# The first stage of an encoder layer: four tiles turned by halves, transposes of the identity put in front, and pieces of work moved from GpSimd to VectorE

## The chip, the core and the metric

The kernel runs on one core of a Trainium2 chip, as one launch. The metric is the device time of a run in microseconds (us). Engines are named as the profile names them: PE (TensorE, matmuls and transposes; PEld is its weight load), DVE (VectorE), ACT (ScalarE), POOL (GpSimd) and SP (SyncE, whose queue issues most DMAs). Each engine takes its instructions in a fixed order; one that waits holds up all that stand behind it on that engine.

## The reference

One layer of a bidirectional encoder on an input of 1024 tokens by 1024 features, in float32: a half-step feed-forward block (SwiGLU, inner width 2816), a token mixer (retention in both directions and a 2-D neighbourhood attention), and a second half-step feed-forward block. Only the first feed-forward block matters here:

```python
h = _swiglu(_rms_norm(x, ffn1_pre_norm[l]), ffn1_w_in[l], ffn1_w_out[l])
x = x + 0.5 * _rms_norm(h, ffn1_post_norm[l])

def _rms_norm(x, gain):
    y = xf * lax.rsqrt(jnp.mean(xf * xf, axis=-1, keepdims=True) + RMS_EPS)
    return (y * gain.astype(jnp.float32)).astype(x.dtype)

def _swiglu(x, w_in, w_out):
    g, u = jnp.split(x @ w_in, 2, axis=-1)
    return (jax.nn.silu(g) * u) @ w_out
```

## The kernel before, in words

**Products.** A float32 product is made of three matmuls of "fp32r" pieces: each operand is split into a high part (a cast on ACT, L62) and a low part (source minus high, a subtraction on DVE, L63); `mm3` (L102 to L104) multiplies high by high, low by high and high by low. One product of a 128 x 512 block by a 512-deep operand is four such triples, 12 matmuls of 512 columns.

**Winograd.** The 1024 x 1024 input (transposed) is cut into four quarters, and a product of it by a block of weights is done with seven products instead of eight: with the operands a11, a12, a22 and the sums s1, s2, s3, s4. `Winograd.put` makes them as the tiles come in: tiles 0 to 3 of 128 tokens give a11 (first half of the features, g = 0) and a12 (second half, g = 1); tiles 4 to 7 give a21 (not kept), a22, s1, s2, s3, and at last s4. In the first stage s4 is made on POOL (L308, L309 and the low part L63 on POOL), four times three instructions of 128 x 512.

**The first stage, in its order.** Eight tiles of 128 tokens are loaded (epx, three buffers), squared and summed on ACT (L126), the root is made on POOL (L112), both halves are scaled on DVE (L132, tile tmp), and each half is turned by four 128 x 128 transposes on PE (L141) into a bank pt, of which there are two. Tiles 0 to 3 are turned as they come. Then `Pairs.lead` runs twelve products a11 and a12 for the first six pairs of weight blocks: six pairs are begun so (three stay in PSUM banks, three are copied to the tile lead). Between them, after every second product, tiles 4 to 7 are turned. Weights are loaded into wraw (three buffers) by SP; the list `(3, 4, 5, 0)` gives the low parts of eight of the twelve weight blocks to POOL.

**The pairs.** Then `ffn_in` runs 22 pairs. `Pairs.run` does for pair i: the subtraction t1 (L421) and t2 (L422) of the weight quarters on DVE, and the products p6 (s2), p2 (a12), p7 (s3), p5 (s1), p4 (a22) and p3 (s4) with the additions between them on DVE (L426, L429, L434, L440, L441, L444, L446). For the first six pairs p1 (a11) and p2 (a12) are there already, so PE has five products of 12 matmuls in each of them, and seven afterwards. `OutSums` (the tile tw) loads blocks of the next weights, subtracts them on DVE (L569) and stores them through POOL's queue; `LeftFactors` makes sums on POOL (L488) and stores them.

**What sets the order.** The code is written as a list of operations. A scheduler places them on the engines by their priorities, and `issue_after`/`after` and the dependency named in `behind` tie some of them to another instruction. The order on each engine is fixed when the program is built.

Of the kernel before, what the change touches and what calls it, by code (L numbers as in the profile page):

```python
# [39 lines left out]
class Core:  # L40
# [74 lines left out]
    def norm_T(self, x, gain, t, pool, put, ss=None, tmps=3):  # L115
# [14 lines left out]
        for b in range(2):  # L130
            bs = slice(b * 512, (b + 1) * 512)
            nc.vector.scalar_tensor_tensor(xn[:, bs], x[:, bs], r[:, 0:1], gain[:, bs], op0=ALU.mult, op1=ALU.mult)  # L132

        return lambda: self.flip([xn[:, :512], xn[:, 512:]], t, put)

    def flip(self, halves, t, put, tag="pt", bufs=2):

        for g, h in enumerate(halves):
            pt = self.bank(tag, bufs)
            for j in range(4):  # L140
                self.nc.tensor.transpose(pt[:, j * P:(j + 1) * P], h[:, j * P:(j + 1) * P], self.ident)  # L141
            f = put(t, g, pt.rearrange("p (k t) -> p k t", k=4))
# [111 lines left out]
class Winograd:  # L254
# [6 lines left out]
    def __init__(self, c, pools, tmp, bufs, spill=None):  # L261

        self.c, self.tmp, self.spill, self.eng, self.late = c, tmp, spill, c.nc.gpsimd, ()
# [11 lines left out]
    def put(self, t, g, pt):  # L275
        c, nc = self.c, self.c.nc
        ts = slice((t % 4) * P, (t % 4 + 1) * P)
        if t < 4:
            c.split(*self.part(("a11", "a12")[g], ts), pt)
            return  # L280
# [7 lines left out]
        if g == 0:  # L288
# [4 lines left out]
            nc.vector.tensor_tensor(self.s3, h1, self.a21, ALU.subtract)  # L293
            nc.vector.tensor_tensor(self.s3, self.s3, l1, ALU.add)
# [12 lines left out]
        if not self.late:  # L307
            self.eng.tensor_tensor(s3, h2, s3, ALU.subtract)  # L308
            self.eng.tensor_tensor(s3, s3, l2, ALU.add)  # L309
            return lambda: c.split(*self.part("s4", ts), s3, eng=self.eng)  # L310
# [26 lines left out]
class Pairs:  # L337
# [3 lines left out]
    def __init__(self, c, x, srcs, held, saved=0, ready=None):  # L341
        self.c, self.x, self.srcs, self.held, self.saved, self.ready = c, x, srcs, held, saved, ready
        self.begun = {}
        self.last = None

    def product(self, a, b, eng=None):
        bank = self.c.bank()
        ah, al = self.x.op(a)
        b = b if isinstance(b, list) else self.c.piece(b, eng)
        for k in range(4):  # L350
            self.c.mm3(bank, [p[:, k * P:(k + 1) * P] for p in b], (ah[:, k], al[:, k]), k == 0, k == 3)
        return bank

# [13 lines left out]
    def lead(self, save=None, between=(), on_pool=(), steps=()):  # L367

        n, done = self.held + self.saved, 0
        for i in (*range(self.held, n), *range(self.held)):  # L370
            if i in self.begun:
                continue
            eng = self.c.nc.gpsimd if i in on_pool else None
            if self.ready is None:
# [5 lines left out]
            for a, w in zip(("a11", "a12"), b):  # L380
                ps.append(self.product(a, w, eng))
                done += 1
                if between and (done in steps if steps else done % 2 == 0):
# [23 lines left out]
    def run(self, i, out, done, sums=None):  # L407
# [16 lines left out]
        late = sums() if sums is not None else []  # L424
        c12 = out(2)
        tt(c12, p6, c11, ALU.add)  # L426
# [7 lines left out]
        self.last = tt(c21, p7, c12, ALU.add).ins  # L434
# [6 lines left out]
        done(3, tt(c12, p5, c12, ALU.add))  # L441
# [3 lines left out]
        p3 = self.product("s4", b22)  # L445
# [1083 lines left out]
```

## Time and profile before

| what | value |
|---|---|
| median of three runs | 2256.53 us (2256.5 to 2257.09) |
| the profiled execution: its own time | 2253.41 us |
| its span, first to last instruction | 2251.6 us |
| PE busy | 2203.2 us, 98% of the span |
| DVE busy | 1677.1 us, 74% |
| ACT busy | 979.2 us, 43% |
| POOL busy | 558.6 us, 25% |

The share of PE is an average. A view by stage tells where PE is not busy: in the first 60 us. A row of the timeline gives start and duration in us, the engine, the line, the operation, what it writes and reads, how many equal ones are merged, and in brackets the idle time before it and what ended it. A matmul's duration is its latency; matmuls overlap, so the distance of two starts is what one costs. L12 is line 12 of the kernel.

### The profile page before, as it was taken

The page shows a single profiled execution, that of the slowest core. Times are in us where ns is not written, and L with a number is a line of the kernel's source. Part 1 is how long each engine was busy: PE and PEld are TensorE (multiplying, and loading weights), DVE is VectorE, ACT ScalarE, POOL GpSimd, SP SyncE. Part 2 cuts the span into 40 slices and gives each one's busy share as a digit, 9 for nine tenths or more (in the row PEclk, how much of TensorE's full clock was granted, in tenths as well). Part 3 has the DMA queues.
Part 4 walks back from the last instruction along what each step waited for, and adds up shares of the span by engine and source line. Part 5 has one row for each costly group of instructions (what it writes and reads, how often), then busy time and mean ns, then how long its engine had stood idle before and what let it go on. Part 6 is the DMA issues. An engine that isn't in the chain of part 4 may idle for free.

```text
span 2251.6 us, 30555 instructions
## 1 busy us (share of the span) xinstructions
PE 2203.2 (98%) x10288; PEld 1834.4 (81%) x10288; DVE 1677.1 (74%) x2941; ACT 979.2 (43%) x2062; POOL 558.6 (25%) x695
## 2 busy tenths in 40 slices
PE   6999999999999999999999999999999999999998
PEld 5888888888887878778888888888788888888886
DVE  7998888855788568869875678534898777776576
ACT  6433333344554222248885675303533332234453
POOL 4343434210121134411101222101124242421012
PEclk9999999999999999999999999999999999999999
DMA  4577787577675542357745477778745454547765
GB/s 168 169 241 277 274 296 266 211 231 236 204 237 191 201 168 99 113 190 243 224 160 178 150 225 241 263 264 297 271 169 187 150 181 147 166 152 239 225 207 180
DMA packets 188014, 466.69 MB, mean 207 GB/s; under 512 B 22417, under 2 KB 50193, under 8 KB 187793
## 3 DMA queue, kind: packets, MB, share of 16 engines
q1 hardware_dynamic: 148944, 334.17, 46.4%
q0 software_dynamic: 38912, 130.58, 14.9%
q8 instruction: 81, 1.33, 0.2%
q14 instruction: 77, 0.62, 0.1%
HBM read 325.72 MB, written 143.13 MB: 208 GB/s over the span
## 4 chain that ended last, share of the span: by engine, by line
PE 85%; DVE 9%; issue 2%; DMA 1%; POOL 1%; ACT 1%; SPq 0%; POOLq 0%; DVEq 0%; ACTq 0%
PE ps L104 26%; PE ps L102 26%; PE ps L103 26%; PE pt L102 1%; PE pt L104 1%; PE pt L103 1%; DVE wl L63 1%; PE ps L806 1%; PE pt L825 1%; POOL rstd L112 1%; DVE t L422 1%; DVE tmp L132 1%; DVE xs L540 1%; PE pt L141 0%; DMA wraw<-in_dram 0%
## 5 line engine op out<-in xcount | busy, mean ns | idle before, releaser
L63 DVE TENSOR_TENSOR wl<-wraw,wh 128x512 fp32r<-128x512 f32 x584 | 426.0, 750 | 53.5 <-ACT wh L62 49.8
L62 ACT CAST wh<-wraw 128x512 fp32r<-128x512 f32 x592 | 345.8, 617 | 204.0 <-DVE wraw L442 89.2
L63 DVE TENSOR_TENSOR gl<-graw,gh 128x512 fp32r<-128x512 f32 (+2 forms) x178 | 129.0, 728 | 163.1 <-ACT gh L62 160.1
L102 PE MATMUL ps<-wh,gh 128*128 128x512 f32 x612 | 239.3, 391 | 0.2 <-DVE tmp L244 0.2
L104 PE MATMUL ps<-wh,gl 128*128 128x512 f32 x612 | 237.3, 390 | 2.0 <-DVE gl L63 1.9
L103 PE MATMUL ps<-wl,gh 128*128 128x512 f32 x612 | 238.3, 389 | 0.0
L62 ACT CAST gh<-graw 128x512 fp32r<-128x512 f32 (+2 forms) x178 | 106.6, 602 | 266.5 <-PE ps L103 99.3
L458 ACT ACTIVATE c<-c 128x512 f32<-128x512 f32 x88 | 55.7, 633 | 265.6 <-DVE c L429 192.5
L104 PEld LDWEIGHTS ps<-wh,gl 128*128 128x128 f32 x612 | 114.7, 188 | 27.1 <-DVE gl L63 3.2
L102 PEld LDWEIGHTS ps<-wh,gh 128*128 128x128 f32 x612 | 114.9, 188 | 24.8 <-DVE tmp L244 1.4
L103 PEld LDWEIGHTS ps<-wl,gh 128*128 128x128 f32 x612 | 114.9, 188 | 23.3
L62 ACT CAST wh<-t 128x512 fp32r<-128x512 f32 x58 | 36.1, 622 | 191.2 <-DVE t L422 178.0
L530 POOL TENSOR_TENSOR q<-q,gain 128x512 f32<-128x512 f32 x22 | 33.5, 1542 | 333.2 <-ACT ps L529 318.5
L102 PE MATMUL ps<-a11h,wh 128*128 128x512 f32 x280 | 111.7, 399 | 0.7 <-ACT a11h L62 0.7
L104 PE MATMUL ps<-a12h,wl 128*128 128x512 f32 x280 | 109.6, 391 | 1.9 <-DVE wl L63 1.9
L104 PE MATMUL ps<-a11h,wl 128*128 128x512 f32 x280 | 110.5, 395 | 0.0
L102 PE MATMUL ps<-a12h,wh 128*128 128x512 f32 x280 | 110.4, 394 | 0.0
L103 PE MATMUL ps<-a11l,wh 128*128 128x512 f32 x280 | 110.2, 394 | 0.0
L102 PE MATMUL ps<-a22h,wh 128*128 128x512 f32 x280 | 109.8, 392 | 0.0
L103 PE MATMUL ps<-a12l,wh 128*128 128x512 f32 x280 | 109.2, 390 | 0.0
L104 PE MATMUL ps<-a22h,wl 128*128 128x512 f32 x280 | 109.1, 390 | 0.0
L103 PE MATMUL ps<-a22l,wh 128*128 128x512 f32 x280 | 109.0, 389 | 0.0
(368 smaller groups left out, 5997.2 us busy)
## 6 DMA issues: line engine op xcount, KB each, us to landing
wraw<-in_dram SPq DMA_DIRECT2D x204, 512.0 KB, 4.5
tw<-in_dram SPq DMA_DIRECT2D x88, 256.0 KB, 3.4
t<-tw POOLq DMA_DIRECT2D x88, 256.0 KB, 4.2
wraw<-t SPq DMA_DIRECT2D x40, 512.0 KB, 3.7
g0s<-cmb POOLq DMA_DIRECT2D x44, 256.0 KB, 5.4
graw<-g0s SPq DMA_DIRECT2D x44, 256.0 KB, 3.1
g1s<-cmb POOLq DMA_DIRECT2D x44, 256.0 KB, 3.9
graw<-g1s SPq DMA_DIRECT2D x44, 256.0 KB, 2.8
```

What stands on the lines that cost most here:

```text
L62: a = nc.scalar.copy(h, src)
L63: self.last = a, (eng or nc.vector).tensor_tensor(l, src, hf, ALU.subtract)
L102: mm(ps, a[0], b[0], start=start, stop=False)
L103: mm(ps, a[0], b[1], start=False, stop=False)
L104: return mm(ps, a[1], b[0], start=False, stop=stop)
L112: self.nc.gpsimd.tensor_tensor(r[:, :n], ms, self.mhalf[:, :n], ALU.pow)
L132: nc.vector.scalar_tensor_tensor(xn[:, bs], x[:, bs], r[:, 0:1], gain[:, bs], op0=ALU.mult, op1=ALU.mult)
L422: tt(t2, b22, t1, ALU.subtract)
L458: a = nc.scalar.activation(gate[j], gate[j], AF.Silu) if j < 2 else None
L530: (eng or c.nc.gpsimd).tensor_tensor(h if out is None else out, h, self.post[:, b * 512:(b + 1) * 512], ALU.mult)
L540: nc.vector.scalar_tensor_tensor(x[:, bs], h, r[:, 0:1], x[:, bs], op0=ALU.mult, op1=ALU.add)
L806: nc.tensor.matmul(bv, q[:, rg * P:(rg + 1) * P], k, start=n == 0, stop=n == 1)
```

## The change

The instructions of the first feed-forward block up to about its seventh pair are changed; all that follows stands in the same order on every engine.

- At the start the first tile is loaded before the gain. 52 transposes of the identity are written ahead of the first tile, and 6 after each of the first three: 70, all into one bank pt that nobody reads (`warm`).
- The first halves of tiles 0 to 3 are scaled and turned first, into four banks of the kind ps (which six products share otherwise); the second halves follow (`early`, `rest`).
- These four banks are kept (`whole`) until tiles 4 to 7 come: s3 starts from the bank with one subtraction (L311) in place of two (before: L293, L294).
- The tiles have four buffers (before: three). The loads of tiles 5 to 7 are written ahead of the second weight block's load. Tiles 6 and 7 are normalised only when tiles 4 and 5 have been turned.
- POOL makes no low part and no s4 any more: all low parts go to DVE, s4 of tiles 4 and 5 to DVE inside pair 0, and s4 of tiles 6 and 7 to DVE inside pair 1 (`s4s`, from s2, with three operations in place of two).
- p3 of pair 0 (s4) is taken out of pair 0 and done after p5 of pair 1 (`hold`, `held`, `tail`).
- Tiles 4 to 7 are turned after products 3, 5, 7 and 9.

In all PE has 70 instructions more, DVE 18 more (8 low parts of weights, 14 for s4, 4 fewer for s3), POOL 20 fewer; ACT and SP have as many as before.

```diff
-        for b in range(2):
+        def scale(b):
             bs = slice(b * 512, (b + 1) * 512)
             nc.vector.scalar_tensor_tensor(xn[:, bs], x[:, bs], r[:, 0:1], gain[:, bs], op0=ALU.mult, op1=ALU.mult)
+        if early:
+            scale(0)
+            self.turn(xn[:, :512], t, 0, put, "ps", 6)
+            def rest():
+                scale(1)
+                self.turn(xn[:, 512:], t, 1, put)
+            return rest
...
+            if g == 0 and self.whole is not None:
+                self.whole[t] = pt
...
-            nc.vector.tensor_tensor(self.s3, h1, self.a21, ALU.subtract)
-            nc.vector.tensor_tensor(self.s3, self.s3, l1, ALU.add)
+            if self.whole is not None:
+                nc.vector.tensor_tensor(self.s3, self.whole.pop(t - 4), self.a21, ALU.subtract)
...
-            self.eng.tensor_tensor(s3, h2, s3, ALU.subtract)
-            self.eng.tensor_tensor(s3, s3, l2, ALU.add)
-            return lambda: c.split(*self.part("s4", ts), s3, eng=self.eng)
...
-        self.last = tt(c21, p7, c12, ALU.add).ins
+        e = tt(c21, p7, c12, ALU.add)
+        self.last = e.ins
+        with c.after((e,)):
+            for f in hold or ():
+                f()
+            if held is not None:
+                held[1]()
...
-        p3 = self.product("s4", b22)
-        done(2, tt(c12, p3, c12, ALU.add))
+        w = c.piece(b22)
+        def tail():
+            p3 = self.product("s4", w)
+            done(2, tt(c12, p3, c12, ALU.add))
...
-        flips = []
-        for t in range(TT):
-            xt = ep.tile([P, D], F32, tag="epx", name="epx", bufs=3)
-            nc.sync.dma_start(xt, x[t * P:(t + 1) * P, :])
-            flips.append(c.norm_T(xt, g, t, ep, wx.put, tmps=4))
-            if t < 4:
-                flips.pop()()
-        fin.lead(lambda: leads.tile([P, 512], F32, tag="lead", name="lead", bufs=6), flips, (3, 4, 5, 0))
+        spin = c.bank("pt", 2)
+        def warm(n):
+            for _ in range(n):
+                nc.tensor.transpose(spin[:, :P], c.ident, c.ident)
+        xs = [load(0)]
+        nc.sync.dma_start(g, g1a)
+        halves = []
+        warm(52)
+        for t in range(4):
+            halves.append(norm(t, xs[t]))
+            warm(6 if t < 3 else 0)
+            xs.append(load(t + 1))
+        fin.fetch(3, 0)
+        for f in halves:
+            f()
+        fin.fetch(3, 1)
+        xs += [load(t) for t in range(5, TT)]
...
+        fin.lead(lambda: leads.tile([P, 512], F32, tag="lead", name="lead", bufs=6), flips, steps=(3, 5, 7, 9))
```

**First place: SP and ACT at the start.** The names: epx is a tile of tokens, wraw a block of weights as loaded, wh its high part, a11h the high part of the first operand, ps and pt banks. Before, on SP, two weight blocks follow the first three tiles, and a third one the fourth:

```order
L1149 DMA epx_169<-in_0_dram 128x1024
L1149 DMA epx_198<-in_0_dram 128x1024
L1149 DMA epx_223<-in_0_dram 128x1024
L79 DMA wraw_317<-in_2_dram 128x1024
L79 DMA wraw_392<-in_2_dram 128x1024
L1149 DMA epx_248<-in_0_dram 128x1024 [waits DMAHW1_49,DVE_49,Activation_49]
L79 DMA wraw_459<-in_2_dram 128x1024
```

Now, on SP:

```order
L1208 DMA epx_293<-in_0_dram 128x1024
L79 DMA wraw_312<-in_2_dram 128x1024
L1208 DMA epx_310<-in_0_dram 128x1024 [waits DMAHW0_49,DVE_49,Activation_49]
L1208 DMA epx_356<-in_0_dram 128x1024 [waits DMAHW2_49,DVE_49,Activation_49]
L1208 DMA epx_358<-in_0_dram 128x1024 [waits DMAHW3_49,DVE_49,Activation_49]
L1208 DMA epx_360<-in_0_dram 128x1024 [waits DMAHW1_49,DMAHW4_49,DVE_49,Activation_49]
L79 DMA wraw_410<-in_2_dram 128x1024
L79 DMA wraw_491<-in_2_dram 128x1024
```

The second weight block (wraw_410) stands behind the loads of tiles 4 to 7, each of which waits until DVE has scaled the tile four before it. And on ACT, now:

```order
L62 CAST wh_352<-wraw_312 128x512
L62 CAST a11h_237<-ps_232 128x4x128 [waits PE_49]
L62 CAST a11h_237<-ps_257 128x4x128 [waits PE_49]
L62 CAST a11h_237<-ps_280 128x4x128 [waits PE_49]
L62 CAST wh_413<-wraw_410 128x512 [waits DMAHW2_49]
L62 CAST a11h_237<-ps_303 128x4x128 [waits PE_49]
L62 CAST a12h_324<-pt_319 128x4x128 [waits PE_49]
```

The high part of the fourth tile's first half (from ps_303), which the first product needs, stands behind the high part of the second weight block.

**Second place: DVE between pair 0 and pair 1.** c0, c1 and gt are the results of pair 0; wraw_802 and wraw_804 (before) or wraw_845 and wraw_847 (now) are the weights of pair 1, and t2 is what its first product p6 reads. Before:

```order
L434 TENSOR_TENSOR c1_682<-ps_713,gt_683 128x512 [waits PE_49]
L421 TENSOR_TENSOR wraw_802<-wraw_804,wraw_802 128x512 [waits DMAHW2_49,DMAHW1_49]
L422 TENSOR_TENSOR t2_806<-wraw_804,wraw_802 128x512 [waits DVE_49]
L431 TENSOR_TENSOR wraw_804<-wraw_804 128x512
L442 TENSOR_TENSOR wraw_802<-wraw_802,t2_806 128x512 [waits DVE_49]
L440 TENSOR_TENSOR gt_683<-ps_731,c1_682 128x512 [waits PE_49]
L441 TENSOR_TENSOR gt_683<-ps_731,gt_683 128x512
L63 TENSOR_TENSOR wl_812<-t2_806,wh_811 128x512 [waits Activation_49]
```

Now:

```order
L460 TENSOR_TENSOR c1_731<-ps_762,gt_732 128x512 [waits PE_49]
L330 TENSOR_TENSOR cmb_435<-a12h_324,cmb_435 128x512
L330 TENSOR_TENSOR cmb_516<-a12h_324,cmb_516 128x512
L331 TENSOR_TENSOR cmb_435<-cmb_435,a12l_325 128x512 [waits DVE_49]
L331 TENSOR_TENSOR cmb_516<-cmb_516,a12l_325 128x512 [waits DVE_49]
L472 TENSOR_TENSOR gt_732<-ps_790,c1_731 128x512 [waits PE_49]
L63 TENSOR_TENSOR s4l_783<-cmb_435,s4h_782 128x4x128 [waits Activation_49]
L63 TENSOR_TENSOR s4l_783<-cmb_516,s4h_782 128x4x128 [waits Activation_49]
L473 TENSOR_TENSOR gt_732<-ps_790,gt_732 128x512
L479 TENSOR_TENSOR c1_731<-ps_810,c1_731 128x512 [waits DVE_49,PE_49]
L444 TENSOR_TENSOR wraw_845<-wraw_847,wraw_845 128x512 [waits DMAHW6_49,DMAHW1_49]
L445 TENSOR_TENSOR t2_849<-wraw_847,wraw_845 128x512 [waits DVE_49]
```

The subtractions for pair 1 stood right behind the sum with p7 of pair 0 (L434); now they stand behind the sum with p4 (L479, bank ps_810). On PE the product that followed p4, p3 of pair 0, is now done inside pair 1, so p6 of pair 1 follows p4 of pair 0.

**Third place: SP between pairs 2 and 3.** wraw_1055 and wraw_1057 (before), wraw_1126 and wraw_1128 (now) are the weights of pair 3; tw are blocks for the sums of the next weights, whose buffers come free when a store of POOL's queue (DMASW) has landed. Before:

```order
L79 DMA wraw_1055<-in_2_dram 128x1024 [waits DMAHW2_49,DMAHW5_49,DVE_49,Activation_49]
L504 DMA graw_4216<-g0a11_78 128x512 [waits DMAHW6_49,DMASW0_49]
L79 DMA wraw_1057<-in_2_dram 128x1024 [waits DMAHW7_49,DMAHW3_49,DVE_49]
L564 DMA tw_1142<-in_3_dram 128x512 [waits DMAHW0_49,DMASW2_49,DVE_49]
L564 DMA tw_1143<-in_3_dram 128x512 [waits DMAHW1_49,DMASW3_49]
L79 DMA wraw_1190<-in_2_dram 128x1024 [waits DMAHW4_49,DVE_49,Activation_49]
L564 DMA tw_1144<-in_3_dram 128x512 [waits DMASW4_49]
L564 DMA tw_1145<-in_3_dram 128x512 [waits DMASW6_49]
```

Now:

```order
L79 DMA wraw_1126<-in_2_dram 128x1024 [waits DMAHW6_49,DVE_49]
L622 DMA tw_1213<-in_3_dram 128x512 [waits DMAHW7_49,DMASW2_49,DVE_49]
L622 DMA tw_1214<-in_3_dram 128x512 [waits DMAHW0_49,DMASW3_49]
L622 DMA tw_1215<-in_3_dram 128x512 [waits DMAHW1_49,DMASW4_49,DVE_49]
L622 DMA tw_1216<-in_3_dram 128x512 [waits DMAHW2_49,DMASW6_49]
L79 DMA wraw_1128<-in_2_dram 128x1024 [waits DMAHW3_49,DVE_49]
```

The second weight block of pair 3 stood ahead of the four tw; now it stands behind them.

104 lines of the change are left out of this document (77 added, 27 removed).

## The prediction

> **What bounds the kernel now.** I read the busy shares by stage first, then PE's timeline for the holes, then what stands ahead of each hole on DVE and SP. The columns of the first view: stretch and its length, then busy time (and instructions) of PE, PEld, DVE, ACT and POOL, granted clock, DMA share, GB/s.
>
> ```profile
> 10.00:20.00 10.00, 4.29 (x17) 2.69 (x16) 8.92 (x12) 7.64 (x18) 8.89 (x8) 1.00 0.73 270
> 20.00:30.00 10.00, 9.32 (x36) 7.51 (x35) 8.09 (x12) 7.50 (x18) 4.53 (x5) 1.00 0.54 164
> 30.00:40.00 10.00, 8.84 (x45) 7.09 (x43) 8.54 (x14) 5.84 (x13) 2.36 (x3) 1.00 0.47 153
> 40.00:50.00 10.00, 6.23 (x32) 4.98 (x32) 8.26 (x14) 6.00 (x12) 5.25 (x3) 0.99 0.16 53
> 61.00:136.00 75.00, 75.00 (x333) 62.08 (x332) 71.96 (x101) 27.89 (x48) 30.62 (x35) 1.00 0.57 191
> ```
>
> Up to 50 us PE has holes. From 61 to 136 us it has none (75.00 of 75), but DVE is busy for 71.96 of the same 75: PE is fed with almost nothing to spare. The change does its good in the first stretch and moves 18 DVE instructions, and several orders, into the second. Now PE's holes:
>
> ```profile
> 19.61 1.97 PE L141 MATMUL pt<-ident,tmp 128*128 128x128 f32 x8 [2.30 <-DVE a12l L63]
> 23.55 0.77 PE L103 MATMUL ps<-a11l,wh 128*128 128x512 f32 x1
> 24.55 0.63 PE L102 MATMUL ps<-a11h,wh 128*128 128x512 f32 x1
> 24.98 0.63 PE L103 MATMUL ps<-a11l,wh 128*128 128x512 f32 x1
> 30.05 1.03 PE L141 MATMUL pt<-ident,tmp 128*128 128x128 f32 x8
> 41.25 0.65 PE L141 MATMUL pt<-ident,tmp 128*128 128x128 f32 x4 [2.41 <-ACT cmb L290]
> 49.68 0.96 PE L141 MATMUL pt<-ident,tmp 128*128 128x128 f32 x4 [2.52 <-ACT cmb L290]
> 50.86 0.63 PE L102 MATMUL ps<-a11h,wh 128*128 128x512 f32 x1
> 53.37 0.39 PE L102 MATMUL ps<-a12h,wh 128*128 128x512 f32 x1
> 53.60 0.39 PE L103 MATMUL ps<-a12l,wh 128*128 128x512 f32 x1
> 67.92 0.39 PE L102 MATMUL ps<-s2h,wh 128*128 128x512 f32 x1
> ```
>
> The second matmul of the first product starts at 23.55, the 145th (the end of the twelve lead products, the start of pair 0) at 67.92. At full clock a matmul costs 53.60 - 53.37 = 0.23 us; behind an idle time of 2.52 us it costs 24.98 - 24.55 = 0.43, as it did at the start (0.63 latency in place of 0.39), until 53.37. So a hole of 2.5 us costs itself and then seven matmuls at 0.2 more, 1.4 us; the one of 2.41 did not. A transpose costs about (30.05 row) 0.1 us warm, (19.61 row) 0.2 cold.
>
> **The start.** SP's queue and the loads, issue by issue:
>
> ```profile
> 0.74 0.38 SPq L1145 DMA_DIRECT2D gpre<-in_dram  x1
> 1.18 1.36 SPq L1149 DMA_DIRECT2D epx<-in_dram  x3
> 5.46 0.63 ACT L126 ACTIVATE tmp<-epx 128x512 f32<-128x512 f32 x1 [3.45 <-DMA epx<-in_dram]
> 7.88 0.63 ACT L126 ACTIVATE tmp<-epx 128x512 f32<-128x512 f32 x1 [1.08 <-DMA epx<-in_dram]
> 9.14 0.63 ACT L126 ACTIVATE tmp<-epx 128x512 f32<-128x512 f32 x1
> 2.59 1.05 SPq L79 DMA_DIRECT2D wraw<-in_dram  x2
> wraw<-in_dram SPq DMA_DIRECT2D x1, 512.0 KB, 7.8
> wraw<-in_dram SPq DMA_DIRECT2D x2, 512.0 KB, 8.1
> 20.88 0.33 SPq L1149 DMA_DIRECT2D epx<-in_dram  x1
> 21.30 0.38 SPq L79 DMA_DIRECT2D wraw<-in_dram  x1
> wraw<-in_dram SPq DMA_DIRECT2D x1, 512.0 KB, 4.4
> ```
>
> Now tile 0 is first and lands about 4.1 (0.74 plus what the gain took, an estimate from the 5.46 of the second load less 1.4 for one load). The rows of a DMA's bytes give the median from issue to landing in the window of that issue (7.8 for the weight block issued at 2.59, 8.1 for it and the next together). Tile 3 is the fifth load behind three tiles and the gain; the fifth of before landed near 10.4 (2.59 + 7.8). Squares of a tile 1.26 (9.14 - 7.88), root and scaling about 2, and on DVE the scaling of tile 2 and a low part in between: the second half of tile 3 is scaled at about 15.8. Only then SP may issue tile 7's load (15.9), and behind it the second weight block (16.3). That lands 4.4 later (the row of 21.30, a weight block right behind a tile) at 20.7; its cast on ACT takes 0.6, and only behind it comes the cast of tile 3's first half, 0.6: first product at 22.0, its second matmul (one low part on DVE later) at 22.7. Against 23.55 that is **-0.9**. The four first halves are turned by about 15; they then lie for 6 us behind one cast that waits for a weight block. Without that wait the first product could start near 16.
>
> The 70 transposes: 52 at 0.2 to 0.1 us are 10.4 to 5.2 us from about 2.4 (identity made). They cost nothing, because PE waits for tiles then, but they buy nothing either: between 16 and 22 PE is idle for longer than the 2.52 us that cost the clock before, so the first product is cold again, as now.
>
> The Trainium skill (TensorE: Matmul & The Clock Gate, Part 4: PE-mode transpose) says that transposes do not count as activity for the gate; Part 1 says that one idle window of about 3.4 us drops the clock. By the first, 70 transposes never warm PE; by the second it is cold at 22 anyhow. The trace agrees with the second as far as 2.52 us of idle time dropped it; the first no row here can show.
>
> **The lead products.** From the second matmul to the 145th are 143 matmuls. Before: 143 x 0.227 = 32.5, 36 transposes 3.9, the holes 2.41 + 2.52, the cold clock some 3: 44.4 = 67.92 - 23.55. Now 40 transposes (4.3), a cold start (2.2), no two holes if DVE keeps up: per tile of 4 to 7 it has 11 instructions at 0.60 (6.6 us) for two products and eight transposes on PE (6.3 us), so some 0.3 is lost: 39.3. The 145th matmul starts at 62.0: **-5.9** in all. If the cover is gone, the holes of 4.9 stay; that is one end.
>
> **Pair 0 to pair 1.** DVE's rows around this place, and POOL's against DVE's:
>
> ```profile
> 73.67 0.68 DVE L434 TENSOR_TENSOR c<-ps,gt 128x512 f32<-128x512 f32 x1
> 74.30 0.69 DVE L421 TENSOR_TENSOR wraw<-wraw 128x512 f32<-128x512 f32 x1
> 75.03 0.69 DVE L422 TENSOR_TENSOR t<-wraw 128x512 f32<-128x512 f32 x1
> 75.64 0.68 DVE L431 TENSOR_TENSOR wraw<-wraw 128x512 f32<-128x512 f32 x1
> 12.04 2.95 POOL L63 TENSOR_TENSOR wl<-wraw,wh 128x512 fp32r<-128x512 f32 x2
> 12.18 1.68 DVE L132 SCALAR_TENSOR_TENSOR tmp<-epx,rstd,gpre 128x512 f32<-128x512 f32 x1
> 13.78 0.68 DVE L63 TENSOR_TENSOR a12l<-pt,a12h 128x512 fp32r<-128x512 f32 x1
> ```
>
> Before, t2 of pair 1 was ready at 75.7, with p5, p4 and p3 of pair 0 (3 x 12 x 0.227 = 8.2 us) still ahead of PE. Now the subtractions stand behind the sum with p4, and p6 of pair 1 follows p4 at once on PE. From p4's last matmul: 0.3 until DVE has it, then three DVE instructions (sum, t1, t2) at 0.6 to 0.7, a cast of 0.6, hand-overs of 0.1 to 0.2: **+3.0**, whatever DVE's backlog. Being longer than 2.52 it costs the clock too: **+1.4**.
>
> **DVE's ledger and pair 2.** DVE gets 18 x 0.60 = 10.8 us more. It gets back what POOL took: while POOL runs, a DVE instruction with both operands in SBUF took 1.68 in place of 0.75 (12.18), one that reads PSUM 0.68 (13.78). Twenty POOL instructions fewer are worth 0 to 20 x 0.93 = 18.6; the two about cancel.
>
> The Trainium skill (GPSIMD Engine Reference, 1. Specifications) says that POOL's SBUF interfaces are shared with VectorE, so that the two hold each other up. The stretched rows agree (1.68 against 0.68); by that rule alone the relief would be at its upper end and DVE free sooner, 18.6 - 10.8 = 7.8 us.
>
> But the work comes in worse places. In pair 1 the six operations for s4 and two low parts stand ahead of pair 2's subtractions, and in pair 2 twelve DVE instructions (sums of pair 0's tail, pair 1's ends, four tw) stand ahead of the low part that p7 needs. 12 x 0.6 = 7.2, one or two stretched by POOL to about 1.2 to 1.7, less the 5 us that p6 and what is left of p3 keep PE busy: 2.2 to 4, I take **+3.0**, and the clock again, **+1.4**.
>
> **Pairs 3 to 5.** The ticks of DVE (its first subtraction of a pair), and SP:
>
> ```profile
> 87.78 0.68 DVE L421 TENSOR_TENSOR wraw<-wraw 128x512 f32<-128x512 f32 x1
> 102.28 1.82 DVE L421 TENSOR_TENSOR wraw<-wraw 128x512 f32<-128x512 f32 x1
> 94.63 0.33 SPq L79 DMA_DIRECT2D wraw<-in_dram  x1
> 100.71 0.92 SPq L564 DMA_DIRECT2D tw<-in_dram  x2
> 101.81 0.33 SPq L79 DMA_DIRECT2D wraw<-in_dram  x1
> 102.19 6.48 SPq L564 DMA_DIRECT2D tw<-in_dram  x2
> ```
>
> Pair 3's second weight block was issued at 94.63, ahead of the four tw. Now it waits for all four, the last of which went at 102.19 + 6.48 = 108.7 less its own 0.3. With 4.4 to land it comes at 110 to 113, when DVE's tick would have been at 102 to 109. Per pair that is 0 (PE still has products) to 6.5 (108.3 - 101.81); with half a pair in hand I take 2, for pairs 3, 4 and 5 **+6**. Afterwards each pair has seven products, 7 x 12 x 0.227 = 19.1 us of PE, and DVE falls behind no more; nothing that follows is reordered, and PE has no slack to win the loss back.
>
> **Sum.** -5.9 + 3.0 + 1.4 + 3.0 + 1.4 + 6 = +8.9. The profiled execution took 2253.41 (span 2251.6 and 1.8 around it), so 2262.3; the median of the runs is 3.1 above it: **2265.4 us**.
>
> **The rivals.**
> - *Only the head counts* (faster). DVE's relief is at the upper end (18.6 - 10.8 = 7.8 us gained), so pair 2 and pairs 3 to 5 cost nothing, and only pair 1's wait stays: -5.9 + 3.0 + 1.4 = -1.5; with the first product at 16 besides, -7.5: 2249 to 2255. For it: the stretched rows. Against: tick and load order, which POOL's relief doesn't touch.
> - *Gain and loss cancel.* Pairs 3 to 5 at 0 and pair 2 at half: about +1, 2257.
> - *Transposes don't warm, and delay.* The 19.61 row shows transposes at 0.2 us each, behind ten microseconds in which PE did scattered transposes. If a run of transposes alone leaves the clock where it was, all 70 and the real ones run at 0.2: 52 until 13, then 18 and 24 more until 22. The first product comes 1 to 1.5 later, and there is one window more at half clock: +2.5, 2268. For it: the 0.2 of the 19.61 row behind 12 us of scattered transposes. Against: that PE was mostly idle then. The rule of the Trainium skill named above (TensorE: Matmul & The Clock Gate, Part 4: PE-mode transpose) would have it so.
> - *The doing does nothing*: the bank that nobody reads is one of two pt banks; it is free when tile 1's second half needs it (about 15), so no price.
>
> **How the numbers follow.** Forecast 0.58, transposes that don't warm 0.19, cancel 0.11, only the head 0.12. What a measurement of this kernel can tell from no change is 0.2%, 4.5 us: faster 0.12, same 0.11, slower 0.77. The forecast's terms have the ends -0.9 (both old holes stay) or -7 at the head, 4.4 for pair 1, 1 to 5.5 for pair 2, 0 to 12 for pairs 3 to 5: about +2 to +16 without all ends at once, 2258 to 2273 for itself. The whole range takes the cancelling case in: 2256 to 2274.
>
> **What would show it.** In the trace after: PE idle from about 15 to 21 with ACT waiting for a weight block; matmul 145 near 62; an idle time of 3 us ahead of the first s2 product of pair 1 released by the cast of t2; one near pair 2's s3 product released by a low part; DVE's first subtraction of pairs 3 to 5 waiting for a load. Wrong it is if PE has no holes between 65 and 140 us, or if the first product starts before 18.

## The result, and the profile after

The changed kernel takes 2272.97 us (median of 6 runs, 2268.36 to 2276.02), the kernel before 2256.52 us: the ratio is 1.0079, with a 95% interval of 1.0067 to 1.0092, that is 15 to 21 us slower. In a second set of runs the ratio was 1.0085 (1.0071 to 1.0099). The forecast was slower by 8.9 us: the direction was right, the size half of what came.

The profiled execution has a span of 2271.3 us, 19.7 more than before. First the busy shares by stage of the changed kernel, with the same columns as in the prediction:

```profile
10.00:20.00 10.00, 4.49 (x36) 3.54 (x33) 7.08 (x13) 3.35 (x9) 1.53 (x2) 0.96 0.80 253
20.00:30.00 10.00, 5.45 (x17) 4.18 (x18) 4.60 (x8) 5.07 (x10) 0.00 (x0) 0.53 0.52 171
30.00:40.00 10.00, 10.00 (x49) 8.34 (x49) 8.83 (x16) 8.00 (x19) 1.47 (x2) 1.00 0.40 120
40.00:50.00 10.00, 9.48 (x48) 7.72 (x47) 9.52 (x18) 7.08 (x15) 0.86 (x1) 1.00 0.55 197
61.00:136.00 75.00, 65.39 (x266) 51.20 (x264) 61.49 (x94) 22.63 (x37) 13.98 (x20) 0.95 0.42 145
```

The change did what it was meant to do between 30 and 50 us: PE is busy for 19.5 of 20 us there (before 15.1). It lost on both sides of that: at 20 to 30 us PE is busy for 5.45 us at a clock of 0.53, and from 61 to 136 us for 65.39 of 75, where it had no hole before. DVE is not fuller there but emptier, 61.49 in place of 71.96. That speaks against DVE's amount of work as the cause; the experiments test it. PE's timeline names the larger holes:

```profile
24.50 0.79 PE L102 MATMUL ps<-a11h,wh 128*128 128x512 f32 x1 [8.39 <-ACT a11h L62]
25.34 0.79 PE L103 MATMUL ps<-a11l,wh 128*128 128x512 f32 x1
79.10 0.50 PE L102 MATMUL ps<-s2h,wh 128*128 128x512 f32 x1 [2.81 <-ACT wh L62]
104.35 0.72 PE L104 MATMUL ps<-s3h,wl 128*128 128x512 f32 x1 [2.75 <-DVE wl L63]
117.97 0.50 PE L102 MATMUL ps<-s2h,wh 128*128 128x512 f32 x1 [1.75 <-ACT wh L62]
133.93 0.50 PE L102 MATMUL ps<-s2h,wh 128*128 128x512 f32 x1 [1.43 <-ACT wh L62]
151.78 0.50 PE L102 MATMUL ps<-s2h,wh 128*128 128x512 f32 x1 [3.01 <-ACT wh L62]
```

A good ruler for what follows is the start of the s2 product of each pair: the same instruction in every kernel, and read off PE's timeline. The table gives it in us for the kernel before, and for the others the difference to it. (In the changed kernel pair 1's s2 has one product fewer ahead of it, p3 of pair 0, which is 2.7 us of PE. So its entry for pair 1 reads 2.7 too low.)

| s2 of pair | 0 | 1 | 2 | 3 | 4 | 5 | 6 | 7 to 11 |
|---|---|---|---|---|---|---|---|---|
| before, at | 67.92 | 81.54 | 95.14 | 108.74 | 122.34 | 135.94 | 152.70 | |
| changed | -2.67 | -2.44 | +2.67 | +9.23 | +11.59 | +15.84 | +17.46 | +17.46 |
| changed, second set | -2.67 | -2.43 | +1.26 | +7.62 | +9.62 | +13.55 | +15.06 | +15.06 |

So the head gained 2.7 us, pairs 0 and 1 together lost 5.3, pair 2 and the wait behind it 6.6 (4.8 and the hole of 1.75 ahead of pair 3), pairs 3 to 5 another 8.2, and from pair 6 on nothing changes any more. That is 17.5 of the 19.7 us. The other 2.2 us came in between two table loads on ACT, which stood 17.1 apart and then 19.3. Before:

```profile
1181.51 1.28 ACT L1325 ACT_TABLE_LOAD   x1
1638.90 1.28 ACT L458 ACT_TABLE_LOAD   x1
```

And in the changed kernel:

```profile
1198.63 1.28 ACT L1416 ACT_TABLE_LOAD   x1
1658.17 1.28 ACT L508 ACT_TABLE_LOAD   x1
```

Nothing is reordered there. The profiles of ten other kernels of this study also lose 0.9 to 5.7 us in that stretch against this one execution of before, even the kernel before with 70 transposes more; so it is read as a difference between executions and not as an effect of the change, though no second profile of the kernel before shows it. The 17.5 us agree with the ratio of the runs (0.0079 x 2256.5 = 17.8). In the second set they do not: its trace has 15.1 us in the first stage, its ratio gives 19.2, and 4.2 lie in the stretch between the two table loads. So a trace and the medians can differ by some 4 us here.

**The head.** The timeline of SP and ACT, changed kernel:

```profile
3.13 0.44 SPq L79 DMA_DIRECT2D wraw<-in_dram  x1
9.23 6.96 SPq L1208 DMA_DIRECT2D epx<-in_dram  x4
16.24 2.69 SPq L79 DMA_DIRECT2D wraw<-in_dram  x3
23.34 0.62 ACT L62 CAST wh<-wraw 128x512 fp32r<-128x512 f32 x1 [9.68 <-DMA wraw<-in_dram]
23.86 0.58 ACT L62 CAST a11h<-ps 128x512 fp32r<-128x512 f32 x1
```

SP holds the second weight block behind tiles 4 to 7 until 16.24. ACT waits 9.68 us for it, and the last first half of tiles 0 to 3 (a11h), which PE had turned by 15.2, is cast behind it. The view of the DMA issues of that moment gives what the load took, in us from issue to landing:

```profile
wraw<-in_dram SPq DMA_DIRECT2D x1, 512.0 KB, 7.1
```

**Pairs 2 to 5.** DVE's timeline: what pair 2's low parts took, and the first subtractions of pairs 3, 4 and 5:

```profile
103.01 3.60 DVE L63 TENSOR_TENSOR wl<-wraw,wh 128x512 fp32r<-128x512 f32 x2
106.54 1.87 DVE L477 TENSOR_TENSOR wraw<-wraw,t 128x512 f32<-128x512 f32 x1
115.79 0.69 DVE L444 TENSOR_TENSOR wraw<-wraw 128x512 f32<-128x512 f32 x1 [3.55 <-DMA wraw<-in_dram]
131.28 0.69 DVE L444 TENSOR_TENSOR wraw<-wraw 128x512 f32<-128x512 f32 x1 [2.89 <-DMA wraw<-in_dram]
149.60 0.69 DVE L444 TENSOR_TENSOR wraw<-wraw 128x512 f32<-128x512 f32 x1 [3.96 <-DMA wraw<-in_dram]
```

All three first subtractions wait for a load, as forecast, and each hole of PE ahead of an s2 product (1.75, 1.43, 3.01) follows one of them.

**What the transposes did.** The view of the tile pt in two windows, 1.4 to 5.0 us and 5.5 to 9.2 us (shortest, median, longest duration in ns):

```profile
L1228 PE MATMUL pt<-ident x17: 421/421/474, 1.4 to 4.8; 128*128 128x128 f32 x17
L1228 PE MATMUL pt<-ident x34: 272/273/384, 5.3 to 9.0; 128*128 128x128 f32 x34
```

And the busy time by stretch when they are over (columns as above):

```profile
16.20:19.40 3.20, 0.00 (x0) 0.00 (x0) 1.98 (x4) 0.00 (x0) 0.00 (x0) 0.96 0.84 261
19.40:24.40 5.00, 0.00 (x0) 0.00 (x0) 0.41 (x1) 1.06 (x3) 0.00 (x0) 0.50 0.80 276
```

The transposes do warm the clock: after some 4 us of them a transpose takes 273 ns in place of 421, and twice as many are done in the same time (17 and then 34, in windows of 3.6 and 3.7 us). The column of the granted clock does not show this step: it reads 1.00 for 1.5 to 4.9 us too, so at the very start it says nothing of a cold PE. But PE then has nothing to do for 8.4 us, the granted clock falls to 0.50 at about 19.1 (the 0.96 of the first row), and the first product runs at half speed. The Trainium skill (TensorE: Matmul & The Clock Gate, Part 4: PE-mode transpose) says that the gate's full clock does not engage for transposes, since they do not count as PE being busy in the same way. These rows, 421 and then 273 ns, do not agree.

### The profile page after: what moved, and what is told of

Same layout as the page of the kernel before. It is cut to its first block, busy times and chain, and to the rows that moved or that the text cites. A ratio compares the mean times of both kernels' runs of the same rounds, so it can differ in the third digit from the quotient of the medians.

```text
span 2271.3 us, 30683 instructions
## 1 busy us (share of the span) xinstructions
PE 2216.5 (98%) x10358; PEld 1843.5 (81%) x10358; DVE 1677.2 (74%) x2959; ACT 979.3 (43%) x2062; POOL 529.1 (23%) x675
## 5 line engine op out<-in xcount | busy, mean ns | idle before, releaser
L63 DVE TENSOR_TENSOR wl<-wraw,wh 128x512 fp32r<-128x512 f32 x592 | 432.9, 752 | 65.1 <-ACT wh L62 61.3
```

The lines of the kernel that those rows point to most:

```text
L63: self.last = a, (eng or nc.vector).tensor_tensor(l, src, hf, ALU.subtract)
```

## The experiments

Each row is the difference of the s2 starts to the kernel before, as above, and then the ratio of the runs to the kernel before with its interval.

| kernel | pair 0 | 2 | 3 | 4 | 5 | 7 | ratio |
|---|---|---|---|---|---|---|---|
| changed | -2.7 | +2.7 | +9.2 | +11.6 | +15.8 | +17.5 | 1.0079 (1.0067 to 1.0092) |
| early_load | -7.0 | -0.8 | +5.3 | +7.6 | +11.7 | +13.6 | 1.0077 (1.0064 to 1.0089) |
| sums_on_pool_queue | -4.3 | +1.1 | +7.7 | +8.4 | +10.7 | +11.0 | 1.0053 (1.0040 to 1.0065) |
| p3_in_pair_0 | -2.6 | 0.0 | +2.0 | +4.4 | +5.7 | +6.1 | 1.0021 (1.0011 to 1.0030) |
| no_transposes | -11.2 | -5.8 | +0.7 | +2.3 | +6.4 | +8.3 | 1.0049 (1.0035 to 1.0062) |
| first_sums_on_dve | -2.7 | +2.4 | +9.1 | +9.1 | +12.1 | +12.4 | 1.0064 (1.0052 to 1.0076) |
| before_with_transposes | +7.6 | +7.6 | +7.6 | +7.6 | +7.6 | +7.6 | 1.0050 (1.0037 to 1.0063) |
| before_pool_work_on_dve | -4.8 | -1.5 | -1.5 | -1.4 | -1.4 | -1.4 | 0.9994 (0.9985 to 1.0003) |
| two_mended_again | -11.2 | -7.5 | -5.3 | -2.9 | -1.7 | -1.3 | 0.9992 (0.9983 to 1.0001) |
| three_mended | -11.2 | -7.6 | -7.6 | -7.2 | -4.9 | -4.5 | 0.9983 (0.9974 to 0.9991) |
| four_mended | -10.8 | -8.3 | -3.8 | -1.5 | -1.5 | -1.6 | 0.9991 (0.9982 to 0.9999) |

The theory under test is that of the prediction: the time is a sum of separate waits, each of them made by what stands in front of something else in a queue. Its main rival: DVE, full from 61 to 136 us before, got 18 instructions too many, and every gain elsewhere is lost to that.

**early_load**: the load alone.

```diff
-                g = self.c.raw(self.srcs[i][0])
+                g = self.raws[i] if i in self.raws else self.c.raw(self.srcs[i][0])
...
+        fin.raws[4] = c.raw(fin.srcs[4][0])
         xs += [load(t) for t in range(5, TT)]
```

> The changed kernel with one load moved: the second weight block (the lead products' second pair) is issued behind tile 4 instead of behind tiles 5, 6 and 7; its two casts then stand ahead of tile 3's first half on ACT, and pair 0's first subtractions come a little earlier on DVE. All that stands behind pair 0 keeps its order. Theory (a sum of separate waits): the 8.4 us in which PE waited for one cast go; first product at about 17 instead of 24.5, warm from the start because PE has turned tiles until 16; the 145th matmul at 58 to 60 instead of 65.3, and all holes behind it stay: 5 to 7 us less than the changed kernel, ratio to the kernel before 1.0048 to 1.0057. Rival (DVE's work is the bound of the whole stage): tiles 4 to 7 come no sooner, the 145th matmul stays near 64, gain under 2 us, ratio 1.007 or more.

Measured: 2270.92 us, ratio 1.0077. The first product starts at 17.18, as the theory had it, and pair 0 comes 4.3 us earlier, not 5 to 7. PE's timeline shows why it is less:

```profile
17.18 0.51 PE L102 MATMUL ps<-a11h,wh 128*128 128x512 f32 x1 [1.10 <-ACT a11h L62]
20.01 0.80 PE L103 MATMUL ps<-a11l,wh 128*128 128x512 f32 x1 [2.33 <-DVE a11l L63]
```

After one matmul PE waits 2.33 us for a low part of a11, which now stands behind the low parts of the weight block on DVE, and the clock is lost in spite of the transposes (0.51 over 19.8 to 23.2 us). In the trace 3.9 of the 4.3 us are still there at pair 7. The run times cannot tell 3.9 us from nothing here (the two intervals overlap almost entirely), so by time this one is inconclusive. By the trace the rival is wrong in its place: tiles 4 to 7 do come sooner, and what is gained at the head is kept.

**no_transposes**: the 70 transposes left out, which no other instruction reads.

```diff
-        warm(52)
...
-            warm(6 if t < 3 else 0)
```

> The changed kernel without the 70 transposes of the identity. Nobody reads them, but the planner counted their time: without them it puts the second and third weight blocks ahead of tiles 5 to 7 by itself and places the first products earlier on ACT and DVE. Theory (the transposes buy nothing, PE is idle long enough behind them to lose the clock): first product at about 16 to 17, its first matmuls at half clock, 145th matmul at 57 to 61; 4 to 7 us less than the changed kernel, ratio 1.0045 to 1.006. Rival (the transposes warm the clock and that is worth something): first product no earlier or colder than now, time the same as or above the changed kernel, ratio 1.0079 or more.

Measured: 2264.90 us, ratio 1.0049, 8 us less than the changed kernel by the medians; in the traces 8.5 at pair 0 and 9.2 at pair 7, so what the head gains is kept. SP's timeline:

```profile
9.29 2.29 SPq L1208 DMA_DIRECT2D epx<-in_dram  x2
11.63 0.90 SPq L79 DMA_DIRECT2D wraw<-in_dram  x2
17.87 0.99 SPq L1208 DMA_DIRECT2D epx<-in_dram  x2
```

and PE's:

```profile
15.88 0.50 PE L102 MATMUL ps<-a11h,wh 128*128 128x512 f32 x1 [1.18 <-ACT a11h L62]
```

Without them the planner, the scheduler that places the instructions, puts the second and third weight blocks ahead of tiles 6 and 7 by itself, and the first product starts at 15.88, 8.6 us earlier. The granted clock is still 1.00 there (13.8 to 17.0 us) and 0.50 from 17.2 to 20.4 us. The transposes are no work that anybody waits for. What they cost comes from the order: with them in the program other instructions are placed elsewhere. That the planner counts their time is only a reading; no run shows how it decides.

**before_with_transposes**: the same 70 in the kernel before, and nothing else.

```diff
+        spin = c.bank("pt", 2)
...
+        warm(52)
...
             if t < 4:
                 flips.pop()()
+                warm(6 if t < 3 else 0)
```

> The kernel before with the 70 transposes of the identity alone (52 ahead of the tiles, 6 behind each of the first three). Theory (they cost through the planner, which counts them and so moves other work): the first product starts at 26 to 34 instead of 22.3, since casts of weights and squares of later tiles now stand ahead of the first tiles on ACT; some of it comes back because tiles 4 to 7 are then ready early; 145th matmul at 70 to 76 (before 67.9), 3 to 9 us slower, ratio 1.0013 to 1.004. Rival (transposes are free and warm the clock): first product at about 22 at full clock, 1.5 us gained, ratio 0.9993 to 1.

Measured: 2265.04 us, ratio 1.0050, above what was expected. PE's timeline:

```profile
22.57 1.12 PE L141 MATMUL pt<-ident,tmp 128*128 128x128 f32 x4 [11.14 <-DVE a11l L63]
34.17 0.79 PE L102 MATMUL ps<-a11h,wh 128*128 128x512 f32 x1
```

PE waits 11.14 us among the tiles and starts its first product at 34.17. Of these 11.9 us, 7.6 are left at pair 0 and stay to the end of the first stage. The runs show 3 to 4 us more; in the profile they lie in the stretch between 1181 and 1639 us named above, and why the runs have them too is open.

**p3_in_pair_0**: the product p3 of pair 0 and s4 of all four tiles put back into pair 0, still all on DVE.

```diff
             held.append(end)
+            for f in held:
+                f()
+            held = None
             continue
```

> The changed kernel with the product p3 of pair 0 and all of s4 put back at the end of pair 0 (DVE still makes all of s4, none on POOL). Theory (p3 was the cover under which DVE prepares pair 1): the hole of 2.81 us ahead of pair 1's s2 product goes, 5.3 us with the clock behind it, and the one of 2.75 us in pair 2, 4.7 us, since pair 2's low part no longer stands behind twelve other instructions: 8 to 12 us less than the changed kernel, ratio 1.0025 to 1.0045, below that if pairs 3 to 5 also gain from it. Rival (18 more DVE instructions are too many wherever they stand): p3 now waits for the last low part of s4, a hole of 3 to 5 us at the end of pair 0, gain under 4 us, ratio above 1.006.

Measured: 2259.55 us, ratio 1.0021, 11.4 us less than the changed kernel at pair 7. PE's timeline has one hole in its place, and DVE's first subtraction of pair 3 comes 7.2 us earlier:

```profile
78.38 0.50 PE L103 MATMUL ps<-s4l,wh 128*128 128x512 f32 x1 [1.76 <-DVE s4l L63]
```

```profile
108.55 0.69 DVE L444 TENSOR_TENSOR wraw<-wraw 128x512 f32<-128x512 f32 x1 [2.86 <-DMA wraw<-in_dram]
```

All the 18 instructions are still on DVE, so the rival falls here. At pair 1 the trace tells the cover from the order: DVE's two subtractions for pair 1 come even later than in the changed kernel (the first at 78.84 in place of 76.94), and yet PE has no hole, because p3 runs meanwhile. So the missing cover made the hole of pair 1. Behind it the edit changes more than one thing: s4 no longer stands ahead of pair 2 on DVE, and on SP a weight block now goes at 102.21, behind two tw loads instead of four. How the gain in pairs 2 and 3 is shared among these is not shown.

**before_pool_work_on_dve**: the ledger by itself. In the kernel before, eight low parts and the 12 instructions for s4 go from POOL to DVE.

```diff
-        self.c, self.tmp, self.spill, self.eng, self.late = c, tmp, spill, c.nc.gpsimd, ()
+        self.c, self.tmp, self.spill, self.eng, self.late = c, tmp, spill, c.nc.vector, ()
...
-        fin.lead(lambda: leads.tile([P, 512], F32, tag="lead", name="lead", bufs=6), flips, (3, 4, 5, 0))
+        fin.lead(lambda: leads.tile([P, 512], F32, tag="lead", name="lead", bufs=6), flips, ())
```

> The kernel before with its 20 POOL instructions of the first stage (8 low parts of weights, 12 of s4) on DVE, no other edit; p3 of pair 0 stays in its pair. Theory (what DVE gets and what it is no longer held up by POOL cancel): lead products a little earlier (145th matmul at 63 to 66 instead of 67.9), p3 of pair 0 waits 1 to 3 us for s4, and from pair 1 on as before: -4 to +2 us, ratio 0.998 to 1.001. Rival (DVE is full from 61 to 136 us, so 12 us more work there is 12 us more time): ratio 1.003 to 1.005.

Measured: 2253.81 us, ratio 0.9994: no difference by time, 1.4 us gained in the trace at pair 7. Pair 0 starts 4.8 us earlier and loses 3.3 of it, but not where it was expected: p3 waits for nothing. PE waits ahead of pair 0 (a row of its timeline, then the busy time of the stretch behind it):

```profile
63.12 0.80 PE L102 MATMUL ps<-s2h,wh 128*128 128x512 f32 x1 [3.04 <-ACT wh L62]
62.70:69.50 6.80, 6.38 (x14) 4.63 (x15) 4.49 (x8) 4.51 (x7) 0.00 (x0) 0.50 0.01 2
```

On DVE t2 of pair 0 stands behind low parts and a sum for s4 there, its cast comes late, and behind the hole the clock is 0.50 for 6.8 us, which are the 3.3 (half of 6.8 is 3.4). So the 20 instructions are felt by PE at one place, and in all the earlier start pays for it.

**sums_on_pool_queue**: tw loads of the second and third set on POOL's queue.

```diff
...
-            self.c.nc.sync.dma_start(t, src[:, k * 512:(k + 1) * 512])
+            (self.c.nc.gpsimd if k in (2, 3) and self.side else self.c.nc.sync).dma_start(t, src[:, k * 512:(k + 1) * 512])
```

> The changed kernel with the second and third set of four tw loads issued from POOL's queue instead of SP's, so that no weight block waits behind them; a few DVE and ACT instructions of pairs 3 to 5 come in another order. Theory (a load queued behind the tw loads): DVE's first subtractions of pairs 3, 4 and 5 wait for no load; the holes ahead of those pairs' s2 products (1.75, 1.43, 3.01 us and the clock behind them) go, so that the 500th matmul, now 17.5 us behind the kernel before, is 8 to 10 behind; 7 to 9 us less than the changed kernel, ratio 1.0040 to 1.0050. Rival (DVE is full there): the subtractions come as late as now for want of DVE, gain under 3 us, ratio 1.0065 or more.

Measured: 2265.11 us, ratio 1.0053, less than expected. Of the 6.4 us that it is ahead at pair 7, 1.6 are there before the edit can act (the second weight block landed in 5.4 us in place of 7.1, and the first product starts at 22.90 in place of 24.50). Pairs 4 and 5 gain 4.8, pair 3 nothing: its first subtraction still waits, 3.56 us.

```profile
114.23 0.69 DVE L444 TENSOR_TENSOR wraw<-wraw 128x512 f32<-128x512 f32 x1 [3.56 <-DMA wraw<-in_dram]
127.89 0.69 DVE L444 TENSOR_TENSOR wraw<-wraw 128x512 f32<-128x512 f32 x1 [1.06 <-DMA wraw<-in_dram]
144.45 0.69 DVE L444 TENSOR_TENSOR wraw<-wraw 128x512 f32<-128x512 f32 x1 [0.73 <-DMA wraw<-in_dram]
```

SP's waits from 100 to 150 us (what it waited for, total, times, longest) tell what holds pair 3's load when no tw stands ahead of it:

```profile
SPq L79 <- DVE wl L63: 46.7, 6, 26.3
```

The load waits for a buffer: there are three for weight blocks, and they come free when DVE has made pair 2's low parts. In the changed kernel too the last of the four tw had been issued by 108.1, and the weight block went only at 109.87.

**first_sums_on_dve**: POOL's first four sums (L546) on DVE.

```diff
...
-        c, eng, j = self.c, self.c.nc.gpsimd, i // 2
+        c, eng, j = self.c, self.c.nc.vector if i == 1 and self.dst is LeftFactors.side else self.c.nc.gpsimd, i // 2
```

> The changed kernel with POOL's first four sums (of pairs 0 and 1, 1.3 to 1.5 us each, at 100 to 108 us) on DVE, so that POOL holds up no DVE instruction there. In the changed kernel the three low parts and the subtraction of pair 2 at 103 to 108 us took 7.9 us in place of 2.4. Theory (part of the unforeseen loss in pairs 2 and 3 is DVE held up by POOL at the very place where pair 2's weight buffers are freed for pair 3's loads): the stretched instructions take 0.6 to 0.7 each; the low part that p7 of pair 2 waits for comes 1 to 2 us later (four sums ahead of it), but the buffers come free 2 to 3 us earlier, the first subtraction of pair 3 is 2 to 3 us earlier and its hole of 1.75 us goes; in all 1 to 4 us under the changed kernel, ratio 1.0062 to 1.0078. Rival (four DVE instructions more are 2.4 us more where DVE is the bound): 2 to 4 us over the changed kernel, ratio 1.009 to 1.0102.

(The expectation counts a row twice: the stretched instructions at 103 to 108 us are two low parts and one subtraction, 3.60 + 1.87 = 5.5 us in place of about 2.) Measured: 2268.00 us, ratio 1.0064, within what the theory gave. DVE's timeline:

```profile
104.62 1.29 DVE L63 TENSOR_TENSOR wl<-wraw,wh 128x512 fp32r<-128x512 f32 x2
105.83 0.69 DVE L477 TENSOR_TENSOR wraw<-wraw,t 128x512 f32<-128x512 f32 x1
112.75 0.69 DVE L444 TENSOR_TENSOR wraw<-wraw 128x512 f32<-128x512 f32 x1 [2.02 <-DMA wraw<-in_dram]
```

The same three instructions take 2.0 us, pair 3's first subtraction comes 3 us earlier, and its hole is gone. The hole in pair 2 grew instead, from 2.75 to 4.06: the low part that it waits for starts at 104.62 in place of 103.01, behind four instructions more. With no sum of POOL beside them the three instructions take 0.6 to 0.7 us each. The Trainium skill (GPSIMD Engine Reference, 1. Specifications) says that POOL's SBUF interfaces are shared with VectorE. These rows agree. The 5.0 us at pair 7 are 2.6 against the second execution of the changed kernel, and the two intervals of the ratio overlap, so the size of the gain is uncertain.

**after_again**, the changed kernel once more.

> The changed kernel once more, beside the other three on one chip, so that differences of 2 to 4 us between variants can be read against it. Both theories: ratio 1.007 to 1.009.

Measured: 2272.84 us, ratio 1.0085. Its row in the first table ends 2.4 us lower. The same hole of 2.81 us ahead of pair 1 may cost the clock or not. In this execution it did not (busy time by stretch; the granted clock is the third number from the end):

```profile
80.00:84.00 4.00, 3.79 (x17) 3.14 (x18) 4.00 (x8) 1.91 (x4) 0.00 (x1) 1.00 0.45 138
```

and in the first one it did:

```profile
80.00:84.00 4.00, 3.80 (x10) 2.99 (x11) 3.16 (x6) 1.90 (x4) 0.00 (x0) 0.57 0.50 149
```

Read so for every hole, the first execution lost the clock behind three of five (0.57 in 4 us behind each of pair 1's, pair 2's and pair 5's, 1.00 behind the 1.75 and 1.43 of pairs 3 and 4). The second lost it behind one (0.60 from 149 to 153 us, behind 2.69 us ahead of pair 5), and not behind 2.81, 2.76 and 2.53 us.

**Two, three and four edits together.** First without transposes and with p3 in pair 0:

> The changed kernel without the 70 transposes and with p3 of pair 0 and all of s4 put back at the end of pair 0: the two edits that gained most alone, together. Theory (separate delays add up): the 8.4 us that the lead products are earlier without the transposes (145th matmul at 56.8 in place of 65.3) and the 13 us that putting p3 back gained add, less what they share (pair 3's weight block, which waits for buffers): 14 to 20 us under the changed kernel, which is 0 to 4 us under the kernel before, ratio 0.998 to 1.0005. Rival (DVE's 18 extra instructions set the pace behind pair 0 whatever the start): the early start is lost by pair 3, ratio 1.002 as with p3 put back alone.

Measured: 2251.79 us, ratio 0.9991 (0.9982 to 1.0000), and once more:

> The kernel with two edits (no transposes, p3 and s4 in pair 0) once more beside the other two and for its profile. Both theories: ratio 0.998 to 1.0.

Measured: 2252.68 us, ratio 0.9992. The two gains of the single edits, 9.2 and 11.4 us at pair 7, would put it at -3.1; it stands at -1.3. The delays add up but for 2 us, which is less than the two executions of the changed kernel differ by.

> The changed kernel without the 70 transposes, with p3 of pair 0 and all of s4 in pair 0, and with the second and third set of tw loads on POOL's queue. Theory (what the loads cost in pairs 4 and 5 is separate): 1 to 3 us under the kernel with the first two edits alone, ratio 0.9975 to 0.999. Rival (with the early start and p3 in its pair the loads are early enough anyway): the same as with two edits, 0.9985 to 0.9997.

Measured, with the two tw sets on POOL's queue besides: 2249.51 us, ratio 0.9983 (0.9974 to 0.9991). It is faster than both kernels, 3.8 us below the kernel before and some 22 below the changed one (by the two ratios). PE's larger holes from pair 0 on:

```profile
69.72 0.50 PE L103 MATMUL ps<-s4l,wh 128*128 128x512 f32 x1 [1.76 <-DVE s4l L63]
125.13 0.50 PE L104 MATMUL ps<-a22h,wl 128*128 128x512 f32 x1 [1.09 <-DVE wl L63]
131.07 0.50 PE L102 MATMUL ps<-s2h,wh 128*128 128x512 f32 x1 [0.65 <-ACT wh L62]
```

> As with three edits, and POOL's first four sums on DVE. Theory (POOL's hold on DVE at 95 to 108 us costs more than four DVE instructions): 0 to 2 us under three_mended. Rival: 2 to 4 us over it.

Measured, with POOL's first four sums on DVE as well: 2252.82 us, ratio 0.9991. Here the rival was right: 3.3 us over three_mended, lost ahead of pair 3 (-7.6 becomes -3.8), where three_mended has no hole. PE's and DVE's timelines:

```profile
104.92 0.50 PE L102 MATMUL ps<-s2h,wh 128*128 128x512 f32 x1 [4.33 <-ACT wh L62]
101.06 0.69 DVE L444 TENSOR_TENSOR wraw<-wraw 128x512 f32<-128x512 f32 x1 [2.00 <-DMA wraw<-in_dram]
103.47 0.68 DVE L445 TENSOR_TENSOR t<-wraw 128x512 f32<-128x512 f32 x1
```

The first low part of pair 2 starts at 94.91, behind the four sums (three_mended: 93.05), the weight block that needs its buffer is issued at 95.67 (94.45), and the first subtraction of pair 3 comes at 101.06 (98.61). Then three other instructions stand between it and the second one, which comes at 103.47 (99.33). So it is the four instructions and an order that came with them; the two were not tried apart. The same edit gained up to 5 us in the changed kernel: what relief is worth depends on what waits behind it.

## Why the prediction was half right

Direction, places and releasers were right; the sum was 8.9 us and the trace has 17.5. The terms that failed are pairs 3 to 5 (+6, measured +10.0) and the head (-5.9, measured -2.7): together 7.2 of the 8.6 us that the sum lacked. By the prediction's own terms:

| term | forecast | measured | where |
|---|---|---|---|
| the head | -5.9 | -2.7 | s2 of pair 0 |
| pair 1, wait and clock | +4.4 | +5.3 | s2 of pair 2 less that of pair 0 |
| pair 2, wait and clock | +4.4 | +4.8 | s2 of pair 3 less its own hole of 1.75 |
| pairs 3 to 5 | +6 | +10.0 | 1.75 + 2.36 + 4.25 + 1.62 |
| sum | +8.9 | +17.5 | s2 of pair 7 |

- **The head: the step that failed is the landing of the second weight block.** Its issue was forecast at 16.3 and came at 16.24. The time to land was taken as 4.4 us, from a row in which one weight block follows one tile; here SP issued three weight blocks in a row behind a tile, and it took 7.1. Other executions with that order had 6.9, 7.2, 6.6 and 5.4 (after_again, p3_in_pair_0, first_sums_on_dve, sums_on_pool_queue), so the order alone does not fix the time, and why it varies is open. The first product came at 24.5 and not at 22.0. That is 2.5 of the 3.2 us; the rest went in the lead products (39.9 us from the second matmul to the 145th, forecast 39.3).
- **The transposes cost nothing: wrong.** As work they cost nothing, and the first product was cold as forecast. But the order in which the second weight block stands behind four tiles exists only because of them: without them the changed kernel is 8 us faster (no_transposes). The prediction read the order that was built and did not ask what had made it. Its rival that transposes don't warm the clock is refuted by 421 and 273 ns.
- **Pair 1** came as described: the hole of 2.81 us, released by the cast of t2, with the two subtractions behind the sum with p4 on DVE. The forecast was 3.0. p3_in_pair_0 shows that the missing cover made it. The 1.4 for the clock was right in one execution and wrong in the other, here and at pair 2: in after_again the two pairs lose 3.9 and 3.8 us, with the clock at 1.00 behind both holes. That a hole longer than 2.52 costs the clock was the prediction's rule, and that it held in the execution of the table is luck.
- **Pair 2** came as described too: 2.75 us, released by a low part behind twelve DVE instructions; forecast 3.0.
- **DVE's ledger** was right in its sum: the two sides cancel (before_pool_work_on_dve, 0.9994), although there PE did wait for DVE at one place, ahead of pair 0.
- **Pairs 3 to 5: right place, half of the mechanism.** Pairs 4 and 5 wait for loads behind the tw loads, and moving those gained 4.8 us. Pair 3's load waited for its buffer, that is for DVE, which was late from pairs 1 and 2 and held up by POOL besides. "Half a pair in hand" was the wrong step: each of the three first subtractions waits for its load (3.55, 2.89 and 3.96 us) and each is followed by a hole of PE, so nothing was in hand. first_sums_on_dve, which leaves SP's order up to pair 3 as it is, moves pair 3's first subtraction by 3.0 us. In p3_in_pair_0 it comes 7.2 us earlier, but there SP's order is another too.

The rivals "only the head counts" and "gain and loss cancel" fell with the holes at 79, 104 and 118 us.

What stays open: what decides whether a hole costs the clock (the length alone does not), why the second weight block takes 5.4 to 7.2 us to land, and the 0.9 to 5.7 us between 1181 and 1639 us. early_load's time did not show the 3.9 us of its trace.

## What to carry to other kernels

An instruction whose result nobody reads can still change where a scheduler places others, so a filler at the start can move loads and casts far behind it: compare the orders with and without it before its effect on the clock is discussed. A product taken out of a pair to spare an engine is also the cover under which the next pair is prepared; ask what stands in its place. And the time that a transfer takes needs a range, taken from rows of a similar order: the same 512 KB load took 4.4 us in the row that was used and 5.4 to 7.2 in five executions.

## What was not expected of the hardware

A run of 128 x 128 transposes back to back sped PE up: 421 ns each up to 4.8 us, 273 ns from 5.3 us on, with the first one at 1.4. In the kernel before, 28 scattered transposes up to 21 us had not done so (0.2 us each at 19.61). After the last transpose, which ended at 16.1, the granted clock fell to 0.50 at about 19.1, some 3 us later. A hole of 2.81 us at the same place cost the clock in one execution (0.57 from 80 to 84 us) and not in another (1.00). Shorter holes did so too: the 1.76 us inside p3 cost it in two_mended_again and three_mended (0.78 from 69 to 73 us) and not in four_mended (1.00 from 70 to 74) or p3_in_pair_0 (1.00 from 78 to 82).
